# Gate vectors, scores and conditioning steps rescheduled in a two-layer mixing and expert kernel

## The chip, the cores and the metric

The kernel runs on one core of one Trainium2 chip. The metric is the device time of one execution in microseconds (us), lower is better. Engines: TensorE (PE; its weight load is PEld), VectorE (DVE), ScalarE (ACT), GpSimd (POOL) and SyncE (SP), which only issues transfers here.

## The reference, cut to what matters

Two layers over 256 tokens `x` and 256 context tokens, model width 1024, float32. In each layer a conditioning vector gives six modulation vectors (shift, scale and gate for the mixing half, the same for the expert half); the hidden state is normed and modulated, mixed (spatial gating beside a bidirectional retention with four heads), gated back into the residual, normed and modulated again, and sent through a mixture of 32 experts, two per token.

```python
def adaln(cond, w_ada, b_ada):
    m = silu(cond) @ w_ada + b_ada                 # 1024 -> 6 x 1024
    return split(m, 6)                             # sh1, sc1, gt1, sh2, sc2, gt2

def hybrid_layer(x, xc, ...):                      # xc only up to the last layer but one
    h = modulate(rmsnorm(x, g_mix), sh1, sc1)
    x = x + gt1 * token_mix(h @ w_in, ...)
    h2 = modulate(rmsnorm(x, g_ffn), sh2, sc2)
    return x + gt2 * hier_moe(h2, ...)

def token_mix(p, ...):
    u, va, q, k, vr, gr, ga, gb = split_projection(p)
    y_a = spatial_gating(gelu(u), gelu(va), ...)
    o = layernorm(retention_bidirectional(q, k, vr, ...))   # per head of 256
    y_b = silu(gr) * o
    return (sigmoid(ga) * (y_a @ w_pa) + sigmoid(gb) * (y_b @ w_pb)) @ w_out
```

## The kernel before

Weights of the mixing half come in pieces of 512 KB (`piece`, `piece_wide`, `piece_qk`, `piece_vg`, lines 237 to 260), one after the other in the order of `plan` (line 556). Each piece is split by `split_w` (line 202) into a rounded high part on ACT (line 206) and a low part on DVE (line 207), and every product is three matmuls (`mm3`, lines 264 to 266). `take` (line 300) keeps three pieces loaded and split ahead of the one in use; the pools of raw, high and low parts have three buffers each. A piece is consumed by a half of `feat_major` or `tok_major` or by a quarter of `tok_wide`, and after each of them `tick` (line 215) is called. `tick` counts, runs the functions that `defer(n, fn)` (line 222) put n ticks ahead, and then pops one conditioning step from `background` unless the count is a multiple of 8 (layer 0) or of 2 (layer 1). Layer 0 has 74 ticks: 4 for the rest of the gating values, 8 for `u`, 16 for `ga` and `w_pa` (ticks 13 to 28), 6 for each of four heads (29 to 52), 16 for `gb` and `w_pb`, 6 for `w_out`.

A conditioning step (`ada_steps`, line 419) multiplies a raw tile of `w_ada` (512 KB) by a column of the conditioning vector and adds it on DVE (line 436), once for each of one or two streams. Raw tiles are requested by the step before (`ada_raw`, line 368): one ahead up to tick 24 and in layer 1, two ahead otherwise in layer 0. Eight steps make one of the twelve vectors (l, v); then a bias row is loaded, four small matmuls sum over partitions (line 445), and vectors 2 to 5 are stored to DRAM from GpSimd's queue (line 460).

In a head, `feat_major` computes q and k, DVE and POOL rotate them (lines 854 to 857), ACT and POOL split them (`split_act`, lines 355 to 357); then `tok_wide` computes the values and the gate gr in four pieces. `scores` is deferred from before `tok_wide`: 2 ticks for head 0 of layer 0, else 1. `values` runs one tick and `back` (the transposes of the head's result) three ticks after `tok_wide`. `values` takes mean and variance of the product in PSUM, 1/sqrt on POOL (`rsqrt`, line 184), normalises on DVE (line 900) and multiplies by silu(gr) on POOL (line 902).

After `w_pb`, `w_out` is applied to two column blocks at once by `tok_wide`, the third by `tok_major`, the fourth tile by tile (`out_tile`, line 1037). For each column block pc, `residual` (line 974) multiplies by the gate vector, adds to the residual, multiplies by the scale and squares. The two vectors come from DRAM, broadcast over partitions, by `mod_slices` (line 536), two tiles in layer 0 and one in layer 1. `route_piece` (line 1003) transposes a block of the result, evicts it on ACT (line 994) and adds the router's logits (line 1000). `pump` (line 272) issues expert weights ahead, in fixed buffers.

PE and SP run their instructions in program order everywhere; DVE, ACT and POOL in program order from the `routing` section on (from the `w_pb` loop), and elsewhere in an order that a planner draws at compile time. SP waits in that order for the buffer of each load. The small tiles of pool t2 share seven buffers, those of a4 seven, those of u4 thirty.

Of the kernel before, what the change touches and what calls it, by code (L numbers as in the profile page):

```python
# [16 lines left out]
AF = mybir.ActivationFunctionType  # L17
# [24 lines left out]
PRE = (({29: 1, 52: 1, 55: 1, 57: 1, 60: 1, 62: 2, 64: 1, 68: 2, 76: 1}, 5, 9),  # L42
       ({4: 1, 8: 2, 12: 1, 18: 1, 33: 1, 38: 1, 47: 1, 50: 2, 58: 1, 59: 1, 60: 1, 61: 1, 63: 1, 65: 1, 73: 1, 74: 1, 75: 1}, 2, 12))
VA_FIRST = [(0, 0), (0, 1), (1, 0), (1, 1), (1, 2), (1, 3), (0, 2), (0, 3)]
RING = (25, 35)
KEPT = [dict(zip((*range(a, a + 5), *range(b, b + 4)), ("raw", "raw", "raw") + 3 * ("whi", "wlo"))) for a, b in ((12, 19), (24, 29))]
KEPT[1].update({8: "a4", 9: "a4", 10: "a4"})
# [4 lines left out]
def hybrid_kernel(  # L52
# [41 lines left out]
    def after(inst, gate):  # L94
        if gate is not None:
            tc.add_manual_dep(inst.ins, gate.ins.name,
                              mybir.DependencyInfo(mybir.DependencyClass.Sync, mybir.DependencyReason.DATA), reason="gate")
# [117 lines left out]
    def tick():  # L215
        ticks[0] += 1
        while deferred and deferred[0][0] <= ticks[0]:
            deferred.pop(0)[1]()
        if background and ticks[0] % (2 if layer[0] else 8):
            background.pop(0)()  # L220

    def defer(n, fn):
# [259 lines left out]
    def ada_planned(vectors):  # L482
        for l, v in vectors:
            background.extend(ada_steps(l, v))
            nexts.extend((l, v, k) for k in range(KD))

    ada_planned([(0, v) for v in range(2, 6)] + [(1, v) for v in range(4)])


    rc = const.tile([P, 2, 36], F32, name="rc")  # L490
# [42 lines left out]

    ms = {}

    def mod_slices(l, pc, gate=None):
        r = []
        for i in range(1 if l == depth - 1 else 2):
            tl = t2t((P, 2, 256))
            after(nc.sync.dma_start(tl, ada_d[l][i].rearrange("(v n) -> v n", v=6)[2:5:2, pc * 256:(pc + 1) * 256].partition_broadcast(P)), gate)  # L540
            r.append(tl)
        return r

# [28 lines left out]
    for l in range(depth):  # L572
# [121 lines left out]
        else:  # L694
# [33 lines left out]
            defer(13, between.close)  # L728
            defer(14, lambda: load_router(1))
            def ada_rest():  # L730
                ada_planned([(1, 4), (1, 5)])
                raws.append(ada_raw(*nexts.pop(0), a4t))

            defer(15, ada_rest)
# [100 lines left out]
        for h in range(HEADS):  # L835
# [45 lines left out]
            def values(scs=scs, yb=yb, vh=vh, vl=vl, gr=gr):  # L881
                st = small([P, 4, 6], tag="ost")
                mv = small([P, 4, 2], tag="omv")
                rs = small([P, 4], tag="ors")
                for s in range(ns):
                    kts = range(4) if s == 0 else range(2)
                    o = bank()
                    for tt in range(2):
                        for kt in kts:
                            sh, sl = (scs[2 * s + kt // 2][:, part, kt % 2, tt * P:(tt + 1) * P] for part in range(2))  # L890
                            vk = kt if s == 0 else 2 + kt
                            mm3(o[:, tt * DV:(tt + 1) * DV], sh, sl, vh[:, vk], vl[:, vk], kt == 0, kt == kts[-1])
                    for tt in range(2):
                        V.bn_stats(st[:, 2 * s + tt], o[:, tt * DV:(tt + 1) * DV])
                        V.bn_aggr(mv[:, 2 * s + tt], st[:, 2 * s + tt])
                    V.tensor_scalar(out=rs[:, 2 * s:2 * s + 2], in0=mv[:, 2 * s:2 * s + 2, 1], scalar1=EPS, scalar2=None, op0=ALU.add)
                    rsqrt(rs[:, 2 * s:2 * s + 2], rs[:, 2 * s:2 * s + 2])
                    for tt in range(2):
                        t = 2 * s + tt
                        V.tensor_scalar(out=yb[:, t], in0=o[:, tt * DV:(tt + 1) * DV], scalar1=mv[:, t, 0:1], scalar2=rs[:, t:t + 1],  # L900
                                        op0=ALU.subtract, op1=ALU.mult)
                        G.tensor_tensor(out=yb[:, t], in0=yb[:, t], in1=gr[:, t], op=ALU.mult)

            def back(h=h, yb=yb):
                for f in range(2):
# [2 lines left out]
                        T.transpose(o[:, t * P:(t + 1) * P], yb[:, t, f * P:(f + 1) * P], ident)  # L908
                    split_act(yT[2 * h + f][0], yT[2 * h + f][1], o[:, 0:nq], V)

            defer(1 if h or last else 2, scores)
            os_, _ = tok_wide(vgj)
            for t in range(4):
                split_act(vh[:, t], vl[:, t], os_[t][:, 0:DV], V)
# [59 lines left out]
        def residual(pc, ts, os_, ms):  # L974
            cs = slice(pc * 256, (pc + 1) * 256)
            for t, o in zip(ts, os_):
                V.tensor_tensor(out=o, in0=o, in1=ms[t // 2][:, 0], op=ALU.mult)
            for t, o in zip(ts, os_):
                done = V.tensor_tensor(out=res[t][:, cs], in0=res[t][:, cs], in1=o, op=ALU.add)
            for t, o in zip(ts, os_):  # L980
                (G if pc < 3 else V).tensor_tensor(out=h2[t][:, cs], in0=res[t][:, cs], in1=ms[t // 2][:, 1], op=ALU.mult)
            for t, o in zip(ts, os_):
                S.activation(o, res[t][:, cs], AF.Square, accum_out=ssq[:, t, pc:pc + 1])
            return done

        def turned(pc, ts):

# [29 lines left out]

        os_, _ = tok_wide([(mT[t // 2], t % 2 * P, 512) for t in range(nt)])
        for pc in range(2):
            done = residual(pc, range(nt), [o[:, pc * 256:(pc + 1) * 256] for o in os_], ms[l, pc])  # L1020
            if pc == 0:
                ms[l, 2] = mod_slices(l, 2, done)
        waiting = []
        defer(1, lambda: waiting.append(route_piece(0)))
        defer(2, lambda: waiting.pop(0)())
# [637 lines left out]
```

## Time and profile before

| | us |
|---|---|
| median of 3 runs | 1876.41 |
| lowest and highest | 1876.13 and 1877.71 |
| profiled execution | 1878.55 |
| its span, first to last instruction | 1876.5 |

In the profiled execution PE was busy for 1806.3 us (96%), PEld 1195.0, DVE 916.4, ACT 582.7 and POOL 405.8. Matmuls are pipelined, and a matmul that runs at half clock is busy for longer, so the share of PE says little about its idles; these are read from its timeline. A row of a timeline gives start, duration, engine, line, operation, output and input, and in brackets the idle of that engine just before and what ended it. Rows of windows give, for a stretch of time, the busy time and instruction count of PE, PEld, DVE, ACT and POOL, the granted clock of PE as a share of full speed, the busy share of the transfer engines and their GB/s.

### The profile page before, as it was taken

To read this page: it belongs to the slowest core of one execution; us is meant where nothing else is said; L and a number is where in the kernel's file an instruction comes from. 1 tells how busy PE (TensorE), PEld (TensorE's weight loads), DVE (VectorE), ACT (ScalarE), POOL (GpSimd) and SP (SyncE) were. 2 spreads that over 40 slices of the span, in tenths; PEclk is the share of its full clock that TensorE was granted. 3 is DMA by queue.
4 is the path that set the end of the run, shared out by engine and by line. 5 is a ranking of instruction groups with operands and counts; after the bars stand their busy time and mean duration, and the time that the engine had idled before them with its cause. 6 is when DMAs were issued, how large, how long until landed. Compare 5 with 4: busy or idle time off the path is not lost. (4 is left out here: it accounts for less than half of the span.)

```text
span 1876.5 us, 26226 instructions
## 1 busy us (share of the span) xinstructions
PE 1806.3 (96%) x9975; PEld 1195.0 (64%) x9975; DVE 916.4 (49%) x1582; ACT 582.7 (31%) x955; POOL 405.8 (22%) x372
## 2 busy tenths in 40 slices
PE   7999998999979999999999899999989999999996
PEld 4888886888875454554544599889964444444442
DVE  4878697774654424333332576755643222223223
ACT  3433233432242221121212365444432222222222
POOL 1021023310030424232333340221021112112121
PEclk8999999999989999999999999989989999999998
DMA  9545453455677999999999478634688999999996
GB/s 348 172 146 201 155 169 124 135 195 198 191 259 282 407 409 408 409 408 409 409 408 407 156 228 288 202 113 144 224 328 342 409 408 409 409 409 409 408 409 252
DMA packets 228468, 553.34 MB, mean 295 GB/s; under 512 B 23633, under 2 KB 106737, under 8 KB 228338
## 3 DMA queue, kind: packets, MB, share of 16 engines
q1 hardware_dynamic: 227954, 551.57, 78.8%
q8 instruction: 80, 1.31, 0.3%
q14 instruction: 50, 0.41, 0.1%
q0 software_dynamic: 384, 0.05, 0.0%
HBM read 550.45 MB, written 1.10 MB: 294 GB/s over the span
## 5 line engine op out<-in xcount | busy, mean ns | idle before, releaser
L1338 POOL TENSOR_TENSOR u<-u,t 128x512 f32<-128x512 f32 x184 | 230.4, 1288 | 720.4 <-DVE t L1337 720.4
L1296 PE MATMUL mm<-u,a 128*64 128x512 f32 x1376 | 334.4, 593 | 2.6 <-ACT a L1211 1.4
L207 DVE TENSOR_TENSOR wlo<-raw,whi 128x1024 fp32r<-128x1024 f32 x159 | 201.3, 1269 | 169.4 <-ACT whi L206 166.9
L266 PE MATMUL mm<-u,wlo 128*128 128x256 f32 (+1 forms) x800 | 268.3, 335 | 1.9 <-DVE wlo L207 1.9
L264 PE MATMUL mm<-u,whi 128*128 128x256 f32 (+1 forms) x800 | 269.8, 337 | 0.0
L1323 DVE SCALAR_TENSOR_TENSOR a<-mm,sw,a 64x512 fp32r<-64x512 f32 x128 | 95.9, 749 | 355.7 <-ACT a L1322 355.5
L265 PE MATMUL mm<-u,whi 128*128 128x256 f32 (+1 forms) x800 | 267.9, 335 | 0.0
L206 ACT ACTIVATE whi<-raw 128x1024 fp32r<-128x1024 f32 x160 | 169.4, 1065 | 259.1 <-PE mm L265 104.8
L1296 PEld LDWEIGHTS mm<-u,a 128*64 128x64 f32 x1376 | 105.8, 137 | 198.2 <-issue 174.2
L264 PE MATMUL mm<-whi,u 128*128 128x512 f32 (+1 forms) x496 | 181.3, 366 | 1.7 <-ACT u L607 1.0
L265 PE MATMUL mm<-wlo,u 128*128 128x512 f32 (+1 forms) x496 | 178.9, 361 | 0.0
L266 PE MATMUL mm<-whi,u 128*128 128x512 f32 (+1 forms) x496 | 178.6, 360 | 0.0
L1300 DVE TENSOR_TENSOR t<-mm,t 64x512 f32<-64x512 f32 x64 | 43.7, 683 | 272.9 <-ACT t L1299 272.9
L266 PEld LDWEIGHTS mm<-u,wlo 128*128 128x128 f32 x800 | 152.2, 190 | 18.1 <-DVE wlo L207 2.7
L1322 ACT ACTIVATE a<-mm,sw 64x512 fp32r<-64x512 f32 x128 | 87.4, 683 | 245.1 <-PE mm L1313 193.7
L264 PEld LDWEIGHTS mm<-u,whi 128*128 128x128 f32 x800 | 152.3, 190 | 17.2 <-issue 1.2
L265 PEld LDWEIGHTS mm<-u,whi 128*128 128x128 f32 x800 | 152.3, 190 | 14.6
L1313 PE MATMUL mm<-u,t 128*64 128x512 f32 x664 | 153.8, 598 | 0.5 <-ACT t L1307 0.5
L1299 ACT ACTIVATE t<-mm 64x512 f32<-64x512 f32 x64 | 38.1, 595 | 296.3 <-PE mm L1296 296.3
L1337 DVE TENSOR_TENSOR t<-mm,u 128x512 f32<-128x512 f32 x190 | 118.5, 675 | 3.4 <-POOL u L1338 3.3
L264 PEld LDWEIGHTS mm<-whi,u 128*128 128x128 f32 x496 | 95.9, 193 | 19.1 <-issue 3.7
L266 PEld LDWEIGHTS mm<-whi,u 128*128 128x128 f32 x496 | 95.2, 192 | 14.3 <-DVE u L609 0.5
(311 smaller groups left out, 2492.3 us busy)
## 6 DMA issues: line engine op xcount, KB each, us to landing
u<-in_w_dram SPq DMA_DIRECT2D x510, 512.0 KB, 10.2
raw<-in_w_dram SPq DMA_DIRECT2D x75, 512.0 KB, 10.2
whi<-in_w_dram SPq DMA_DIRECT2D x73, 512.0 KB, 9.6
wlo<-in_w_dram SPq DMA_DIRECT2D x73, 512.0 KB, 8.8
raw<-in_w_in_dram SPq DMA_DIRECT2D x64, 512.0 KB, 5.1
a<-in_w_ada_dram SPq DMA_DIRECT2D x52, 512.0 KB, 6.1
raw<-in_w_in_dram SPq DMA_DIRECT2D x96, 256.0 KB, 3.1
u<-in_w_ada_dram SPq DMA_DIRECT2D x44, 512.0 KB, 5.9
```

The costliest lines, as they stand in the source:

```text
L206: S.activation(hi, rv, AF.Copy)
L207: low_by[0].tensor_tensor(out=lo, in0=rv, in1=hi.bitcast(F32), op=ALU.subtract)
L264: T.matmul(out, lhsT=sh, rhs=mh, start=first, stop=False)
L265: T.matmul(out, lhsT=sh, rhs=ml, start=False, stop=False)
L266: return T.matmul(out, lhsT=sl, rhs=mh, start=False, stop=last)
L1296: T.matmul(o[h * 64:(h + 1) * 64, :], lhsT=x[:, s0:s0 + 64], rhs=w(k), start=(k == 0), stop=(k == KD - 1), tile_position=(0, 64 * h))
L1300: V.tensor_tensor(out=hh[0:64], in0=o[0:64, :], in1=hh[0:64], op=ALU.mult)
L1313: T.matmul(o[n % banks][n * 64:(n + 1) * 64, :], lhsT=hTt[:, s], rhs=wc(s)[:, n * 512:(n + 1) * 512], start=(s == 0), stop=(s == 3), tile_ ...
L1322: S.activation(dh, src, AF.Copy, scale=w)
L1323: V.scalar_tensor_tensor(out=dl, in0=src, scalar=w, in1=dh.bitcast(F32), op0=ALU.mult, op1=ALU.subtract)
L1337: V.tensor_tensor(out=y, in0=o, in1=g2[t // 2][:, hs], op=ALU.mult)
L1338: eng.tensor_tensor(out=res[t][:, hs], in0=res[t][:, hs], in1=y, op=ALU.add)
```

## The change

Four edits. (1) `scores` is always deferred by 2 ticks. (2) In `values` DVE subtracts the mean and multiplies by silu(gr) in one operation that reads PSUM, and ACT multiplies by 1/sqrt afterwards; POOL's multiply goes. (3) The gate and scale vectors of the third column block are loaded from GpSimd's queue after both first residuals; before, SP's queue loaded them with a wait on the first residual. (4) In layer 0 the number of conditioning steps at each tick comes from a table `ADA`, and vector (1, 2) is computed in layer 1.

```diff
+ADA = {t: 1 for t in (*range(1, 8), *range(9, 29), *(29 + 6 * h + i for h in range(4) for i in (1, 4, 5)), *range(53, 61), *range(61, 70, 2))}
+ADA.update({16: 2, 20: 2, 24: 2, 28: 2})
@@ def tick
-        if background and ticks[0] % (2 if layer[0] else 8):
+        for _ in range(min(len(background), ticks[0] % 2 if layer[0] else ADA.get(ticks[0], 0))):
             background.pop(0)()
@@
-    ada_planned([(0, v) for v in range(2, 6)] + [(1, v) for v in range(4)])
+    ada_planned([(0, v) for v in range(2, 6)] + [(1, v) for v in (0, 1, 3)])
@@ def mod_slices
-    def mod_slices(l, pc, gate=None):
+    def mod_slices(l, pc, eng=None):
-            after(nc.sync.dma_start(tl, ada_d[l][i].rearrange(...)[2:5:2, pc * 256:(pc + 1) * 256].partition_broadcast(P)), gate)
+            (eng or nc.sync).dma_start(tl, ada_d[l][i].rearrange(...)[2:5:2, pc * 256:(pc + 1) * 256].partition_broadcast(P))
@@ def ada_rest
-                ada_planned([(1, 4), (1, 5)])
+                ada_planned([(1, 2), (1, 4), (1, 5)])
@@ def values
-                        V.tensor_scalar(out=yb[:, t], in0=o[:, tt * DV:(tt + 1) * DV], scalar1=mv[:, t, 0:1], scalar2=rs[:, t:t + 1],
-                                        op0=ALU.subtract, op1=ALU.mult)
-                        G.tensor_tensor(out=yb[:, t], in0=yb[:, t], in1=gr[:, t], op=ALU.mult)
+                        V.scalar_tensor_tensor(out=yb[:, t], in0=o[:, tt * DV:(tt + 1) * DV], scalar=mv[:, t, 0:1], in1=gr[:, t],
+                                               op0=ALU.subtract, op1=ALU.mult)
+                        S.activation(yb[:, t], yb[:, t], AF.Copy, scale=rs[:, t:t + 1])
@@
-            defer(1 if h or last else 2, scores)
+            defer(2, scores)
@@ output projection
         for pc in range(2):
-            done = residual(pc, range(nt), [o[:, pc * 256:(pc + 1) * 256] for o in os_], ms[l, pc])
-            if pc == 0:
-                ms[l, 2] = mod_slices(l, 2, done)
+            residual(pc, range(nt), [o[:, pc * 256:(pc + 1) * 256] for o in os_], ms[l, pc])
+        ms[l, 2] = mod_slices(l, 2, G)
```

## Rows read from the trace of the kernel before

**Rows 1.** The page: PE's busy tenths and transferred GB/s in forty slices of 46.9 us

```profile
PE   7999998999979999999999899999989999999996
GB/s 348 172 146 201 155 169 124 135 195 198 191 259 282 407 409 408 409 408 409 409 408 407 156 228 288 202 113 144 224 328 342 409 408 409 409 409 409 408 409 252
```

**Rows 2.** Timeline of PE, 260 to 320 us (layer 0, heads 0 and 1), main idles

```profile
282.54 0.33 PE L908 MATMUL mm<-ident,u 128*128 128x128 f32 x1 [0.87 <-POOL u L902]
...
290.23 0.58 PE L264 MATMUL mm<-u,u 128*128 128x256 f32 x1 [5.24 <-ACT u L356]
291.58 0.58 PE L266 MATMUL mm<-u,u 128*128 128x256 f32 x1 [0.55 <-POOL u L357]
293.26 0.58 PE L264 MATMUL mm<-u,u 128*128 128x256 f32 x1 [0.46 <-DVE u L357]
```

**Rows 3.** Timeline of PE, 1178 to 1295 us (layer 1, heads), main idles

```profile
1219.12 0.39 PE L264 MATMUL mm<-u,u 128*128 128x256 f32 x1 [1.59 <-ACT u L356]
1220.47 0.38 PE L266 MATMUL mm<-u,u 128*128 128x256 f32 x1 [0.85 <-POOL u L357]
...
1254.34 0.39 PE L264 MATMUL mm<-u,u 128*128 128x256 f32 x1 [1.37 <-ACT u L356]
1256.10 0.58 PE L266 MATMUL mm<-u,u 128*128 128x256 f32 x1 [1.26 <-POOL u L357]
```

**Rows 4.** Timeline of PE, output projection of layer 0 and of layer 1

```profile
528.85 3.63 PE L1000 MATMUL mm<-wr,t 128*128 128x36 f32 x16 [3.64 <-ACT t L994]
...
1377.04 1.92 PE L1000 MATMUL mm<-wr,t 128*128 128x36 f32 x8 [5.00 <-ACT t L994]
```

**Rows 5.** Windows of 5 us behind these idles: after the busy times, PEclk, transfers

```profile
290.00:295.00 5.00, 3.76 (x14) 3.17 (x15) 3.85 (x5) 2.10 (x4) 1.58 (x2) 0.50 0.25 72
530.00:535.00 5.00, 5.00 (x28) 4.12 (x28) 3.34 (x7) 1.06 (x1) 0.51 (x1) 0.50 0.96 222
1223.00:1228.00 5.00, 5.00 (x26) 4.26 (x25) 3.04 (x6) 3.40 (x5) 0.13 (x1) 0.83 0.32 95
1257.00:1262.00 5.00, 5.00 (x17) 4.23 (x17) 3.94 (x7) 3.16 (x4) 0.00 (x0) 0.50 0.79 254
1376.00:1381.00 5.00, 3.96 (x19) 3.96 (x20) 3.91 (x7) 2.58 (x6) 0.51 (x1) 0.50 1.05 406
```

**Rows 6.** Timelines of POOL and ACT, layer 0, head 1

```profile
281.75 1.41 POOL L902 TENSOR_TENSOR u<-u,u 128x256 f32<-128x256 f32 x2 [0.72 <-DVE u L900]
...
289.55 0.63 ACT L356 ACTIVATE u<-t 128x512 fp32r<-128x512 f32 x1 [3.59 <-POOL t L857]
```

**Rows 7.** Window 130 to 235 us, ticks 13 to 28; its costliest DVE group

```profile
130.00:235.00 105.00, 105.00 (x504) 86.19 (x504) 77.28 (x101) 34.17 (x39) 10.88 (x12) 0.98 0.52 173
...
L436 DVE SCALAR_TENSOR_TENSOR u<-u,cst,u 128x1024 f32<-128x1024 f32 x25 | 34.2, 1399 | 0.0
```

**Rows 8.** Line 900: duration in ns, min/median/max

```profile
L900 DVE TENSOR_SCALAR u<-mm,omv,ors x24: 533/540/548, 277.1 to 1311.7; 128x256 f32<-128x256 f32 x24
```

**Rows 9.** Waits of SP's queue: us in total, times, longest

```profile
SPq L540 <- DVE mm L977: 19.0, 1, 19.0
SPq L540 <- DVE u L979: 9.6, 1, 9.6
```

**Rows 10.** Timeline of ACT, output projection of layer 0 and of layer 1

```profile
527.25 1.06 ACT L206 ACTIVATE whi<-raw 128x1024 fp32r<-128x1024 f32 x1 [7.75 <-DMA raw<-in_w_out_dram]
...
1375.45 1.06 ACT L206 ACTIVATE whi<-raw 128x1024 fp32r<-128x1024 f32 x1 [5.51 <-DMA raw<-in_w_out_dram]
```

**Rows 11.** POOL's timeline at 515 us; the page's transfer issues (KB, us to landing)

```profile
515.20 5.61 POOL L981 TENSOR_TENSOR u<-u,t 128x256 f32<-128x256 f32 x8 [44.75 <-DVE u L979]
...
u<-in_w_ada_dram SPq DMA_DIRECT2D x44, 512.0 KB, 5.9
...
ada<-t POOLq DMA_DIRECT2D x12, 4.0 KB, 2.9
```

More of the change, by code (lines that the diff above doesn't have):

```diff
@@ L539, in mod_slices @@
             tl = t2t((P, 2, 256))
-            after(nc.sync.dma_start(tl, ada_d[l][i].rearrange("(v n) -> v n", v=6)[2:5:2, pc * 256:(pc + 1) * 256].partition_broadcast(P)), gate)
+            (eng or nc.sync).dma_start(tl, ada_d[l][i].rearrange("(v n) -> v n", v=6)[2:5:2, pc * 256:(pc + 1) * 256].partition_broadcast(P))
             r.append(tl)
@@ L978, in residual @@
             for t, o in zip(ts, os_):
-                done = V.tensor_tensor(out=res[t][:, cs], in0=res[t][:, cs], in1=o, op=ALU.add)
+                V.tensor_tensor(out=res[t][:, cs], in0=res[t][:, cs], in1=o, op=ALU.add)
             for t, o in zip(ts, os_):
@@ L983, in residual @@
                 S.activation(o, res[t][:, cs], AF.Square, accum_out=ssq[:, t, pc:pc + 1])
-            return done
         def turned(pc, ts):
```

## The prediction

> **What bounds the kernel now.** I read the forty slices of the page first [rows 1]. Two regimes alternate. In the expert stages the transfers run at a flat 408 to 409 GB/s, slice after slice; nothing but fewer bytes would shorten these stretches, and the change moves hardly any bytes. In the two mixing stages (about 60 to 560 us and 1070 to 1400 us) the transfers run far below that, and TensorE is at nine tenths or more in nearly every slice. There TensorE is the bound, and the stage can only lose its idles and its slow clock. The saturated weight stream starts when the mixing stage hands over its buffers and the first expert starts, so I take a microsecond saved in either mixing stage as a microsecond of the total. Second, TensorE's timeline, only the rows with an idle in brackets: layer 0's heads [rows 2], layer 1's heads [rows 3], the output projection of both layers [rows 4]. Third, the granted clock just after those idles [rows 5]: 0.50 of full speed, that is 1.2 of 2.4 GHz, in three 5 us stretches that follow an idle of several us. So an idle costs twice: itself, and the half speed behind it.
>
> **Part 1, scores one piece later** (line 911 of the kernel before). [Rows 2] shows the idle at head 1 of layer 0: 0.87 before the transposes of head 0's result, then 5.24, 0.55 and 0.46 before head 1's scores, 7.1 us. Behind the 5.24 is a chain over ACT and POOL [rows 6]: POOL is at the old gating until 283.2, then it adds the rotary halves, and ACT's first score operand comes at 289.55. The 5 us from 290 had 3.76 us of TensorE work at 0.50, which is 1.9 us lost. In layer 1 [rows 3] has 1.59 + 0.85 at head 1 and 1.37 + 1.26 at head 2, 5.1 us; the clock costs 0.17 x 5 = 0.85 and 0.50 x 5 = 2.5, 3.4 us [rows 5]. The other heads waited for under 1 us.
> The change puts one more piece of matmuls ahead of the scores. A piece is 24 matmuls; 504 took 105 us [rows 7], 0.21 each, so a piece is 5.0 us in layer 0. In layer 1 half of a value piece's matmuls are 256 wide: about 3.8 us. Against the waits: 7.1 - 5.0 leaves 2.1 in layer 0, from which part 2 takes its share; 2.4 and 2.6 are below 3.8, so layer 1 is covered. What is late next would be the values, which need the scores' evictions: three pieces of cover remain (15 us; over 11 in layer 1). Head 0 of layer 0 has had the later place all along, and its values show no row in [rows 2]. Gain if all goes: 7.1 + 1.9 + 5.1 + 3.4 = 17.5 us. Lower end: 5.0 of the 7.1, the clock still low there, layer 1 whole: 13.5.
>
> **Part 2, values gated from PSUM** (lines 900 to 902). Per half tile of 128x256, 24 in all, it removes one DVE tensor_scalar of 0.54 us [rows 8] and one POOL multiply (two took 1.41 [rows 6], 0.7 each), and adds one DVE scalar_tensor_tensor from PSUM and one ACT copy with a scale. The trace has no scalar_tensor_tensor of exactly these operands; the same operation on 128x1024 took 1.40 [rows 7], a quarter of that is 0.35, and the removed form is 0.54. I take 0.5 (nearest in size and source), so DVE keeps its time: 24 x (0.5 - 0.54) = -1 us, between -4.6 and +1, none of it on TensorE's path alone. ACT gets 24 copies no longer than the 0.63 of a 128x512 one [rows 6]: at most 15 us in all, beside matmuls. What matters is order: DVE no longer waits for POOL's square root before it can free the bank, and POOL loses 2.8 us per head of layer 0 just ahead of the rotary adds. That is worth up to 2 us of the 2.1 left at head 1. Behind ACT's new wait for the square root stand the weight splits; they are three pieces ahead, so I cost the wait at nothing (0 to 1 us per head if that cover is gone).
>
> **Part 3, gate vectors through GpSimd's queue** (lines 540 and 1020 to 1022). The old load sits on SP's queue, which goes in program order, with a gate on the first residual. SP stood there 19.0 us in layer 0 and 9.6 in layer 1 [rows 9]. Queued behind it are the last w_out pieces. ACT's split of such a piece then waited 7.75 and 5.51 for its data [rows 10], the eviction of the router's transposes stands behind that split on ACT, and TensorE waited for that eviction 3.64 and 5.00 [rows 4]. The clock after: 0.50 x 5 = 2.5 in layer 0 and 0.50 x 3.96 = 2.0 in layer 1 [rows 5]. Gain: 3.6 + 5.0 + 2.5 + 2.0 = 13.1 us. SP's pumps of expert weights behind the gate also start some us earlier; they only refill a ring that is full before the experts start, so I count nothing.
> What it costs: three 256 KB loads (two in layer 0, one in layer 1) are now queued on POOL behind both residuals' multiplies, which in layer 0 ended at 520.8 [rows 11]. For a 256 KB load from that queue no row exists. Its bounds: the 4 KB ones landed after 2.9 us, a 512 KB load on SP's queue after 5.9 [rows 11]. I take 4.5. So in layer 0 the vectors are there at about 526.5, DVE and POOL need some 4 us for the third residual, and TensorE, freed of its idle, asks for it at about 529 to 530: 0 to 3 us late, I take 1. In layer 1 everything has half the length and half the cover: 0 to 4, I take 2. Behind the POOL instruction stands only the next residual's multiply.
> The Trainium skill speaks against this part: "DMA: Bandwidth & Descriptors", section on issuing engines that are not separate DMA queues, says that spreading issue over engines saves only the sequencer's issue time. By that rule the 13.1 would be near zero. The trace of before does not agree with it here, since SP's 19.0 us was a semaphore wait with other loads behind it, not issue.
>
> **Part 4, conditioning steps by stage** (lines 219, 487, 731). Counting ticks (one per piece, 74 in layer 0): ticks 13 to 28 get 20 steps instead of 14, the heads (29 to 52) 12 instead of 21, the rest 24 instead of 29; vector (1, 2), eight one-stream steps, goes to layer 1. A two-stream step is two DVE operations of 1.40 [rows 7], 2.8 us. So the heads lose 9 x 2.8 = 25 us of DVE work, which shortens the chain of part 1, and ticks 13 to 28 gain 6 x 2.8 = 17 us. DVE was busy 77.3 of 105 us there [rows 7], idle 27.7: it fits. But at ticks 16, 20 and 24 the second step takes a raw tile just requested, which lands 5.9 us later [rows 11], and DVE goes in order. 3 x 5.9 + 17 = 35 against 27.7: about 7 us of lateness, spread, against splits three pieces (15 us) ahead. I take 1 us on TensorE's path, bounds 0 and 8. The steps' loads move with them, 512 KB each, on SP's queue, past weight pieces; the transfers are at half load there, no cost. Layer 1 gains 8 x 1.4 = 11 us of DVE work and one small store on POOL's queue, in a stage with DVE idle: nothing.
>
> **The sum.** Gains 17.5 + 13.1 = 30.6. Given back: gate vectors late 1 + 2, double steps 1, and 2 for what part 1 leaves at head 1 or for a tile of the seven-deep t2 pool that head 0 now shares with a bias row: 6. Net 25. The profiled execution took 1878.55 us (span 1876.5 and 2.05 around it), 0.1% above the median of the runs, 1876.41; I subtract from the median: **1851.4 us**; a profile of the changed kernel would show a span near 1851.
>
> **The rivals.** (a) The gate vectors land late, or their new queue saves nothing: the output stage keeps its 13.1, heads as forecast: 1876.4 - 17.5 + 3 = 1862. (The Trainium skill's rule in part 3 would end here.) For it: no row of such a load on POOL. Against: even at 5.9 us the lateness is smaller than the idle removed. (b) The heads keep their waits, because the chain is late by DVE's order rather than by place, or because evictions come too late for the values; the output stage gains: 1876.4 - 13.1 + 3 = 1866. Against: waits of 2.4 to 2.6 us under 3.8 us of cover. (c) Slower: DVE becomes the bound in ticks 16 to 28. If at each of the three single-look-ahead double ticks the in-order wait runs as long as the queue's slow landings, about twice 5.9, and all of it reaches TensorE with the added 2.8: 3 x (11.8 + 2.8) = 44, less 6 that the sum already gives back: 1851.4 + 38 = 1889. It decides against the change from about 10 us of TensorE idle per double tick. For it: DVE at 74% there before. Against: the three-piece lead must be eaten each time. (d) The saved time is swallowed because the weight stream, not TensorE, sets the hand-over: within 0.2%. Against: the slices before each expert stage run at 113 to 342 GB/s [rows 1].
>
> **How the numbers follow.** Forecast 0.60, (a) 0.14, (b) 0.11, (c) 0.06, (d) 0.05, a better case 0.04: nothing given back, 1876.4 - 35 with the small idles and low-clock stretches that I left out = 1841. The range runs from 1841 to 1867, so it takes in (a) and (b) and leaves out (c), (d) and odd ends. A measurement of this kernel can tell about 0.2% (3.8 us) from no change. Faster by more than that: 0.60 + 0.14 + 0.11 + 0.04 = 0.89, less 0.02 for mixtures: 0.87; within: 0.06; slower: 0.07.
>
> **What would show it.** Right: no idle above 1 us before the scores in either layer, no row of SP waiting at the gate vectors' line, no idle of 3 to 5 us before the router's logits, granted clock 1.00 through the heads. Wrong: DVE waiting for w_ada tiles near 150 to 230 us with idle rows on TensorE's line 266; DVE waiting for the gate vectors before the third residual; ACT waiting for POOL's square root with a weight split behind it. The prediction fails most easily if the compiler's order of DVE, ACT and POOL, which is drawn anew outside the hand-ordered parts, opens an idle elsewhere, since an idle of 3 us costs about 5.

## The result and the profile after

The changed kernel takes 1858.18 us (median of 4 runs, 1857.55 to 1860.08) against 1877.06 for the kernel before in the same session: a ratio of 0.9895, 95% interval 0.9875 to 0.9915. That is 19 us faster, where 25 were forecast. The time lies inside the range, but it was not reached in the way of the forecast.

To see where the time went I cut both spans at the same instructions of TensorE's timeline: the first transposes for the router, the start of the experts, and their ends (us; the marks of each stage are read from the timeline).

| stage | before | after | difference |
|---|---|---|---|
| start | 44.70 | 43.73 | -1.0 |
| layer 0, mixing up to the router | 473.70 | 461.62 | -12.1 |
| layer 0, output stage | 45.48 | 49.16 | +3.7 |
| layer 0, experts | 500.26 | 500.42 | +0.2 |
| layer 1, mixing up to the router | 303.92 | 293.02 | -10.9 |
| layer 1, output stage | 32.27 | 30.56 | -1.7 |
| layer 1, experts to the end | 476.17 | 478.49 | +2.3 |
| span | 1876.5 | 1857.0 | -19.5 |

A stage can move by some 3 us without an edit in it. In the kernel with part 3 alone, described below, the mixing of layer 0 took 477.23 us and that of layer 1 300.94, 3.5 more and 3.0 less than before, though that edit stands in the output stages and the idles in the heads stayed nearly the same. What differed is the granted clock. From 150 to 200 us, where TensorE was busy throughout in both kernels, it was 0.93 against 0.97, from 250 to 300 us 0.90 against 0.93, from 1065 to 1115 us 0.93 against 0.97 and from 1215 to 1265 us 1.00 against 0.90, which adds up to about these 3.5 and 3.0 us. The sum of both mixing stages was steadier: 778.2 against 777.6.

**The heads.** The page of the changed kernel has the same two regimes as [rows 1]; PE's tenths no longer fall near 290 us, and the dip left in layer 0 is that of the output stage (here PE and GB/s in the forty slices).

```profile
PE   7999999999969999999999899999989999999996
GB/s 346 179 144 226 183 137 125 147 205 167 150 224 303 407 409 408 408 408 409 408 408 407 171 209 299 206 173 213 248 331 339 409 409 409 409 409 409 409 409 251
```

Windows of the changed kernel at the places of [rows 2, 3], with the columns of [rows 5]:

```profile
282.00:287.00 5.00, 5.00 (x27) 4.21 (x26) 2.62 (x3) 2.56 (x4) 2.04 (x3) 1.00 0.68 211
287.00:292.00 5.00, 5.00 (x32) 4.51 (x31) 4.83 (x7) 1.79 (x2) 0.00 (x0) 1.00 0.32 103
1215.00:1220.00 5.00, 5.00 (x30) 4.37 (x29) 3.16 (x6) 4.42 (x6) 0.00 (x0) 1.00 0.34 110
1250.00:1255.00 5.00, 5.00 (x41) 4.84 (x40) 3.87 (x7) 4.84 (x9) 1.29 (x1) 1.00 1.02 341
```

PE is busy for the whole of each window and the granted clock is 1.00. No idle of 0.35 us or more is left in the heads of either layer.

**The output stage.** TensorE still waits before the router's logits, in layer 0 for twice as long as in [rows 4], in layer 1 for less (timeline of PE):

```profile
524.87 3.63 PE L1002 MATMUL mm<-wr,t 128*128 128x36 f32 x16 [7.25 <-ACT t L996]
...
1360.47 1.08 PE L1002 MATMUL mm<-wr,t 128*128 128x36 f32 x8 [2.87 <-ACT t L996]
```

The reason is a new one. In the timelines of POOL, DVE and ACT, and in the view of line 543 (the load of the vectors, line 540 before):

```profile
506.25 1.55 POOL L543 DMA_DIRECT2D t<-ada  x2
...
517.92 0.77 DVE L980 TENSOR_TENSOR mm<-mm,t 128x256 f32<-128x256 f32 x2 [3.73 <-DMA t<-ada]
521.52 0.76 DVE L980 TENSOR_TENSOR mm<-mm,t 128x256 f32<-128x256 f32 x2 [2.83 <-DMA t<-ada]
...
522.63 0.39 ACT L986 ACTIVATE mm<-u 128x256 f32<-128x256 f32 x1 [14.61 <-DVE u L982]
524.25 1.05 ACT L996 ACTIVATE t<-mm 128x512 f32<-128x512 f32 x2
...
1350.26 0.81 POOL L543 DMA_DIRECT2D t<-ada  x1
1357.91 0.76 DVE L980 TENSOR_TENSOR mm<-mm,t 128x256 f32<-128x256 f32 x2 [3.38 <-DMA t<-ada]
...
DMA to landing us min/median/max: 7.6/11.7/14.4
```

POOL issues the loads of layer 0 from 506.25 on; they land 11.7 and 14.4 us after their issue, the one of layer 1 after 7.6, and DVE waits for them in the third residual. ACT squares that residual, and behind the squares, in ACT's program order, stands the eviction (line 996) of the second block's transposes, which have nothing to do with the third block. So TensorE waits. SP's row of [rows 9] is gone, and another has come at the same line:

```profile
SPq L543 <- POOL u L984: 13.9, 2, 12.9
```

SP now stands 12.9 us at the next load, the vectors of the fourth block, for a buffer of the t2 pool that POOL still reads. In the window from 496 to 504 us the transfers moved 2 GB/s.

### The profile page after: what moved, and what is told of

It is laid out like the page before. It is cut to its first block, busy times and chain, and to the rows that moved or that the text cites. A ratio compares the mean times of both kernels' runs of the same rounds, so it can differ in the third digit from the quotient of the medians.

```text
span 1857.0 us, 26227 instructions
## 1 busy us (share of the span) xinstructions
PE 1798.0 (97%) x9975; PEld 1190.8 (64%) x9975; DVE 916.7 (49%) x1582; ACT 590.9 (32%) x979; POOL 386.3 (21%) x351
## 5 line engine op out<-in xcount | busy, mean ns | idle before, releaser
L209 ACT ACTIVATE whi<-raw 128x1024 fp32r<-128x1024 f32 x160 | 169.5, 1065 | 203.0 <-PE mm L268 82.3
```

The lines of the kernel that those rows point to most:

```text
L209: S.activation(hi, rv, AF.Copy)
```

## The experiments

My theory after the result: (1) part 1 makes the gain; (2) part 3 costs in layer 0, because its load lands late; (3) parts 2 and 4 matter little. The rivals: that the parts need each other, that the queue is what is slow, that other loads in flight are, and that the load itself is. Stage times are taken at the marks of the table.

**Part 3 taken back.** The changed kernel with the load on SP's queue again:

```diff
...
+            done = residual(pc, range(nt), [o[:, pc * 256:(pc + 1) * 256] for o in os_], ms[l, pc])
+            if pc == 0:
+                ms[l, 2] = mod_slices(l, 2, done)
-        ms[l, 2] = mod_slices(l, 2, G)
```

> The changed kernel with part 3 taken back: the third block's gate vectors are again loaded by SP's queue behind a gate on the first residual. Theory (in the changed kernel the load from GpSimd's queue landed 7.6 to 14.4 us after its issue, so part 3 only moved the output projection's idle): the idles of before come back, about 3.6 us at the router's logits in layer 0 and 5.0 in layer 1, in place of 7.25 and 2.87, with about the same half-speed clock behind them; total 1854 to 1860, no more than 4 us from the changed kernel. Rival (part 3 gains what the prediction gave it, and something else lengthened the output stage): 10 us slower, about 1868.

Measured: 1854.6 us (1851.66 to 1855.84), ratio 0.9866 (0.9842 to 0.9889). That is 3.6 us faster than the changed kernel, though the intervals overlap. SP's waits and the old idles (timeline of PE) are back, the first of them smaller:

```profile
SPq L543 <- DVE mm L980: 19.6, 1, 19.6
SPq L543 <- DVE u L982: 9.7, 1, 9.7
...
515.59 1.98 PE L1003 MATMUL mm<-wr,t 128*128 128x36 f32 x16 [2.46 <-ACT t L997]
1352.73 1.93 PE L1003 MATMUL mm<-wr,t 128*128 128x36 f32 x8 [5.03 <-ACT t L997]
```

The output stage takes 42.54 us in layer 0 (49.16 with part 3) and 32.34 in layer 1 (30.56). So beside the other parts, part 3 costs 6.6 us in layer 0 and gains 1.8 in layer 1. How much it costs depends on part 4, as the kernel without part 4 shows below.

**Part 1 alone**, in the kernel before:

```diff
-            defer(1 if h or last else 2, scores)
+            defer(2, scores)
```

> The kernel before with part 1 alone: scores one piece later in every head. Theory (the place of the scores is what removed the heads' idles): no idle over 1 us before the scores in either layer, 17 to 22 us faster than before, about 1857. Rival (the DVE load of the conditioning steps delays the chain, and dealing them out otherwise is what helped): idles of 2 us and more stay at head 1 of layer 0, under 10 us faster, 1868 to 1874.

Measured: 1863.82 us (1862.89 to 1866.71), ratio 0.9923 (0.9900 to 0.9946), 15 us gained, under the 17 to 22 expected. The mixing of layer 0 takes 466.86 us (6.8 less) and that of layer 1 293.22 (10.7 less). In layer 0 small idles remain at head 1 (timeline of PE), the last two of them before its values; in layer 1 none remain:

```profile
279.76 0.33 PE L908 MATMUL mm<-ident,u 128*128 128x128 f32 x1 [0.54 <-POOL u L902]
288.84 0.38 PE L266 MATMUL mm<-u,u 128*128 128x256 f32 x1 [0.72 <-POOL u L357]
290.52 0.39 PE L264 MATMUL mm<-u,u 128*128 128x256 f32 x1 [0.94 <-DVE u L357]
...
311.28 0.39 PE L265 MATMUL mm<-u,u 128*128 128x256 f32 x1 [0.71 <-DVE u L357]
312.80 0.39 PE L265 MATMUL mm<-u,u 128*128 128x256 f32 x1 [0.91 <-DVE u L357]
```

**All but part 1**, the same edit undone in the changed kernel:

```diff
-            defer(2, scores)
+            defer(1 if h or last else 2, scores)
```

> The changed kernel with part 1 taken back: scores one piece after q and k, but for head 0 of layer 0. Theory (place): the idles come back in layer 1 whole, 5 us and their clock, and in layer 0 in part, 3 to 7 us; 10 to 18 us slower than the changed kernel, 1868 to 1876. Rival (DVE load and POOL's share of the chain): under 5 us slower, below 1863.

Measured: 1875.21 us (10 runs, 1873.12 to 1876.62), ratio 0.9979 (0.9968 to 0.9990). Without part 1 almost nothing is gained. Yet the mixing of layer 0 is 9.9 us shorter (463.79), while that of layer 1 is 5.3 us longer (309.18), with a new idle at head 0 (timeline of PE):

```profile
282.43 0.39 PE L267 MATMUL mm<-u,u 128*128 128x256 f32 x1 [1.00 <-ACT u L359]
...
1182.03 0.39 PE L267 MATMUL mm<-u,u 128*128 128x256 f32 x1 [3.15 <-ACT u L359]
1184.07 0.58 PE L269 MATMUL mm<-u,u 128*128 128x256 f32 x1 [1.54 <-POOL u L360]
```

Heads 2 and 3 of layer 1 wait too, 2.0 and 1.8 us. So most of the wait at head 1 of layer 0 goes in two ways: by a later place (part 1), or by a shorter chain (parts 2 and 4). Layer 1 needs the later place. What opens the idle at its head 0 was not tried; part 4 moves eight conditioning steps into this layer, which the prediction costed at nothing.

**Part 4 taken back, and part 2 taken back**, each alone, in the changed kernel; the diffs are those of the change, reversed, in `tick` and in the lists of vectors, and in `values`.

> The changed kernel with part 4 taken back: conditioning steps by the old rule, vector (1, 2) again in layer 0. Theory (part 4 shortened layer 0's heads by taking DVE work out of them and the output stage of layer 0 by ending the steps before it, and did nothing in ticks 13 to 28): 3 to 6 us slower than the changed kernel, 1861 to 1864, with idles of 0.5 to 1 us each at heads 1 and 2 of layer 0, none in layer 1. Rival (part 4 is neutral or its double steps and layer 1's extra steps cost as much as they give): within 2 us of 1858.

> The changed kernel with part 2 taken back: normalised on DVE, multiplied by the gate on POOL. Theory (with the scores a piece later and less DVE work in the heads nothing waits for this chain): within 2 us of the changed kernel, 1856 to 1860. Rival (POOL's multiplies ahead of the rotary adds still set the scores): idles of 0.5 us and more before the scores or the transposes, 4 to 8 us slower, 1862 to 1866.

Measured: 1860.27 us without part 4 (1857.26 to 1862.57, ratio 0.9904, 0.9887 to 0.9920) and 1859.23 without part 2 (1855.17 to 1861.22, ratio 0.9898, 0.9881 to 0.9914). Neither can be told from the changed kernel. The mixing of layer 0 takes 462.55 and 460.06, against 466.86 with part 1 alone. Beside part 1, part 4 removes all the small idles; part 2 removes those before the transposes and the scores and leaves two before head 1's values, 1.02 and 0.91 us. Without part 4, TensorE also waits elsewhere in the output stage of layer 0 (timeline of PE):

```profile
306.51 0.39 PE L268 MATMUL mm<-u,u 128*128 128x256 f32 x1 [1.02 <-DVE u L360]
521.43 0.69 PE L469 MATMUL mm<-ident,t 128*128 128x128 f32 x2 [5.34 <-DVE t L452]
```

That stage takes 46.10 us, 3.1 less than in the changed kernel. The last conditioning vector still falls into it, and SP stands at the load of its bias row (line 366) until after POOL has issued the gate vectors. So GpSimd's load goes first, lands after 6.0 and 8.5 us, and DVE doesn't wait for it in layer 0. With part 4 the fourth block's vectors stand there instead, SP issues them before POOL's load, and that load lands after 11.7 and 14.4. Part 4 thus takes idles out of the heads and makes part 3 dearer.

**The load early, in another pool, on SP's queue.** The third block's vectors get tiles of the a4 pool and are requested right behind the second `w_out` piece of that block, without a gate; nothing is on GpSimd's queue.

```diff
-        if kh and pc == 3:
-            ms[l, pc] = mod_slices(l, pc)
+        if kh:
+            ms[l, pc] = mod_slices(l, pc, a4t if pc == 2 else t2t)
-        ms[l, 2] = mod_slices(l, 2, G)
```

> The changed kernel with the third block's gate vectors in buffers of pool a4 instead of t2, loaded by SP's queue behind the second w_out piece of that block, with no gate and nothing on GpSimd's queue. Theory (what held SP before, and what made the load late after, is that no t2 buffer is free before the first residual; with another buffer the load is early and nobody waits for it): no wait of SP over 5 us at this line, no wait of DVE for it, no idle over 1 us before the router's logits in either layer; 9 to 14 us faster than the changed kernel, 1844 to 1849. Rival (the output stage's idles come from the saturated transfers or from the order on ACT): idles of 3 us and more stay, 1855 to 1860.

Measured: 1842.88 us (1842.03 to 1843.65), ratio 0.9806 (0.9784 to 0.9827): 15 us below the changed kernel, 36 below the kernel before. The output stages take 38.44 and 26.36 us. What is left of the idles at the router's logits and transposes (timeline of PE) and of SP's waits:

```profile
518.14 1.97 PE L1002 MATMUL mm<-wr,t 128*128 128x36 f32 x16 [0.50 <-ACT t L996]
1338.40 0.44 PE L993 MATMUL mm<-ident,u 128*128 128x128 f32 x2 [1.60 <-POOL u L984]
...
SPq L543 <- DMA ada<-t: 6.8, 1, 6.8
SPq L543 <- POOL u L984: 2.3, 1, 2.3
```

The gain that part 3 was forecast to bring exists; it comes once the vectors are there in time (requested at 482.32, DVE doesn't wait for them). SP's wait has not gone: both waits shown stand before the fourth block's vectors in layer 0, 9.1 us together where the changed kernel had 12.9, so the expectation of no wait over 5 us was wrong. Those vectors were issued at 499.50 and 502.17, and that was early enough.

**Why did the load land late? First the queue.** The load from ACT's queue instead of GpSimd's, at the same place of the program:

```diff
-        ms[l, 2] = mod_slices(l, 2, G)
+        ms[l, 2] = mod_slices(l, 2, S)
```

> The changed kernel with the third block's gate vectors issued from ACT's queue instead of GpSimd's, at the same place in the order. Theory (what is slow is not the kind of queue but the broadcast and its company): 8 to 14 us to landing in layer 0, 6 to 9 in layer 1, total within 4 us of the changed kernel. Rival (GpSimd's queue itself is slow with loads of this size): 3 to 6 us to landing, idles before the router's logits under 2 us, 5 to 9 us faster.

Measured: 1848.43 us (one run). ACT issued the loads 2 us sooner, at 504.22 and 504.72, since it didn't stand behind POOL's multiplies. DVE used the second one at 515.34, and in layer 1, issued at 1339.4, it waited until 1348.44 (timeline of DVE):

```profile
515.34 0.76 DVE L980 TENSOR_TENSOR mm<-mm,t 128x256 f32<-128x256 f32 x2 [0.58 <-DMA t<-ada]
1348.44 0.76 DVE L980 TENSOR_TENSOR mm<-mm,t 128x256 f32<-128x256 f32 x2 [4.71 <-DMA t<-ada]
```

Nine to eleven us on this queue too, so GpSimd's queue alone is not what makes the load slow. But it had a share: the output stage of layer 0 took 39.11 us instead of 49.16. Neither expectation came whole: the landing is the theory's, the gain of 10 us more than the rival's. The transfers from 506 to 508 by queue (q10 is ACT's, q1 SP's):

```profile
q10 hardware_dynamic: 226, 0.22, 33.1%
q1 hardware_dynamic: 140, 0.13, 28.3%
```

ACT's load moved beside the one in SP's queue, each at its own low rate. GpSimd's load, in the changed kernel, had its first packet only after 512, when SP's 512 KB of vectors had nearly gone.

**The weights in flight.** The pump of expert weights moved behind the output tiles, meant to keep them away from the load:

```diff
         sh2.append(tl)
-        pump(PRE[l][1])
...
-        pump(PRE[l][2])
+        pump(PRE[l][1] + PRE[l][2])
```

> The changed kernel, but the pump of expert weights that stands behind the third residual is moved behind the router's part of the output stage, so that SP issues no stream of 512 KB weight loads beside the gate vectors. Theory (the load from GpSimd's queue lands late because it shares the transfer engines with that stream): it lands within 3 to 6 us of its issue in both layers, where the changed kernel needed 11.7 and 14.4 in layer 0 and 7.6 in layer 1. Rival (broadcast loads from one row of DRAM are slow by themselves; in the changed kernel the transfers ran at 26 to 92 GB/s just after 504 us with the engines 0.1 to 0.3 busy): 9 us and more in layer 0 still. The total is of little interest, since expert weights start later.

Measured: 1854.65 us (one run), landing 8.0 to 14.3 us, DVE's waits 10.2 us. This decides nothing: SP has no other work between the two places and issued the same loads at the same moment, at 504.76, as before the edit. The weights alone were not tried again.

**What is read.** The vectors are one row of DRAM, read once for each of 128 partitions. In the next kernel GpSimd's load takes 128 distinct rows of x, pieces of the same length (the third block is then gated and scaled by rows of x); in the one after it, the two loads of the shift vector do.

```diff
-            (eng or nc.sync).dma_start(tl, ada_d[l][i].rearrange(...)[2:5:2, ...].partition_broadcast(P))
+            if eng is None:
+                nc.sync.dma_start(tl, ada_d[l][i].rearrange(...)[2:5:2, ...].partition_broadcast(P))
+            else:
+                eng.dma_start(tl, x_d[0, 0:P].rearrange("p (v n) -> p v n", v=4)[:, 0:3:2])
```

> The changed kernel, but the load on GpSimd's queue takes its 256 KB from 128 distinct rows of x instead of one row of the conditioning vectors read 128 times; the pieces have the same length. The third column block is therefore gated and scaled by wrong values. Theory A, many reads of the same DRAM row are slow by themselves: the load lands in 3 to 6 us instead of 7.6 to 14.4, DVE's 10 us of waiting for the vectors falls to under 3, the output stage of layer 0 shortens by 5 to 7 us, and the time is about 1851. Theory B, the load is slow because of what else is in flight then (the broadcast loads and weights that SP issues at the same moment): landing stays at 8 us or more, DVE still waits 7 us or more, time within 3 us of the changed kernel's 1858.

> The changed kernel, but the two 512 KB loads of the shift vector, which SP issues in the output stage at the same moment as GpSimd's load is under way, take distinct rows of x instead of one row read 128 times. The shift added before the experts is therefore wrong. Theory A (a load is slow by its own repeated reads): the gate vectors still land in 8 to 14 us, DVE waits 8 us or more, time about 1858. Theory C (broadcast loads hold each other up, since they read from the same few rows): the gate vectors land in 4 to 8 us, DVE's wait halves, the output stage of layer 0 shortens by 3 to 5 us and the time is about 1853. Theory B (any company does it): no change, as in A.

Measured: 1853.0 and 1859.24 us (one run each). With distinct rows for GpSimd's load it landed after 11.0 and 11.7 us in layer 0 and 7.6 in layer 1, and DVE waited 7.2 us (10 before); the output stage of layer 0 took 46.44 us, 2.7 less. With the shift alone nothing moved (landing 8.0 to 14.2, wait 10.1). So GpSimd's load is not slow by its own reads alone, and the shift's loads are not what holds it up.

**Part 3 alone**, in the kernel before:

> The kernel before, with the third part of the change alone: the gate vectors of the third block through GpSimd's queue behind both first residuals. The prediction's sum: 1877 less 13.1 plus 3 for lateness, 1867. The reading of the runs so far, that the load lands 8 to 14 us after its issue and DVE then waits for it: the idles before the router's logits in layer 0 go, but the third residual is late by as much; output stage of layer 0 from 45.5 to 48 to 52, of layer 1 from 32.3 to about 30.5, time 1877 to 1882, no faster than before.

Measured: 1878.81 us (10 runs, 1876.92 to 1881.26), ratio 0.9992 (0.9982 to 1.0001): nothing gained. The output stages took 46.18 and 31.40 us, 0.7 more and 0.9 less than before. In layer 0 the idle before the router's logits is gone, but another has come (timeline of PE), with SP's waits from 496 to 530 us:

```profile
536.42 0.69 PE L466 MATMUL mm<-ident,t 128*128 128x128 f32 x2 [5.95 <-DVE t L449]
...
SPq L363 <- DVE mm L977: 11.1, 1, 11.1
SPq L363 <- POOL t L362: 7.9, 1, 7.9
```

SP stood 19.0 us at line 363, the bias row of the last conditioning vector. The last `w_out` piece was queued behind it, DVE stood 9.55 us for the split of that piece, and the conditioning step that TensorE waited for stood behind it on DVE. For the gate vectors DVE did not wait in layer 0; in layer 1 it did, 4.1 us. So in layer 0 the idle went as expected, but the stage grew by less and for another reason: the third residual was held up by SP's next wait, not by the landing.

In layer 0 this kernel shows the load with the transfer engines nearly to itself. Its issue on POOL's timeline, then the transfers from 522.7 to 531 by queue (packets, MB, busy share of the 16 engines; q0 is GpSimd's, q1 SP's), then line 540 (the 8.4 is layer 1's):

```profile
522.71 1.57 POOL L540 DMA_DIRECT2D t<-ada  x2
...
q0 software_dynamic: 154, 0.52, 71.9%
q1 hardware_dynamic: 108, 0.11, 4.3%
...
DMA to landing us min/median/max: 6.3/8.4/8.5
```

In a cut of the same view by single microseconds the first packets come after 524, so some 1.5 us pass up to there, and the 512 KB then take until 531: some 75 GB/s with hardly any company. The 4.5 us of the prediction could not have held even here.

**All vectors from distinct rows**, on SP's queue as on GpSimd's, gate, scale and shift (all three are then rows of x):

```diff
-    (eng or nc.sync).dma_start(tl, ada_d[l][i].rearrange(...)[2:5:2, ...].partition_broadcast(P))
+    (eng or nc.sync).dma_start(tl, x_d[0, 0:P].rearrange("p (v n) -> p v n", v=4)[:, 0:3:2])
-            nc.sync.dma_start(tl, ada_d[l][i, 3 * D:4 * D].partition_broadcast(P))
+            nc.sync.dma_start(tl, x_d[0, 0:P])
```

> The changed kernel, but every load of gate and scale vectors, on SP's queue and on GpSimd's, and both loads of the shift vector take distinct rows of x instead of one row read 128 times, with pieces of the same length. The residuals are therefore gated, scaled and shifted by wrong values. In the traces so far the 512 KB of the fourth block's vectors, first in SP's queue from 504 us on, moved at 58 to 88 GB/s, and the first packet of GpSimd's load came only about 6 us after its issue. Theory A, one row read 128 times is what is slow: from 504 on SP's queue moves over 200 GB/s, GpSimd's load has its first packet within 3 us and lands within 6, DVE waits under 4 us in all, the output stage of layer 0 takes 40 to 43 us instead of 49, and the time is about 1849. Theory D, the slowness comes from the size of the pieces (1 KB) or the crowd after 504, whatever is read: SP's queue still moves 58 to 100 GB/s up to 510, the landing stays at 8 us or more, DVE waits 7 us or more, and the time is 1852 to 1858.

Measured: 1846.72 us (one run), output stage of layer 0 38.54 us instead of 49.16. The windows from 504 to 510, first of the changed kernel, then of this one (last column GB/s, before it the busy share of the transfer engines):

```profile
504.00:506.00 2.00, 2.00 (x19) 2.00 (x18) 0.21 (x2) 1.97 (x8) 2.00 (x4) 1.00 0.20 58
506.00:508.00 2.00, 2.00 (x19) 2.00 (x18) 1.38 (x1) 2.00 (x3) 1.79 (x3) 1.00 0.33 84
508.00:510.00 2.00, 2.00 (x19) 2.00 (x18) 1.23 (x1) 0.02 (x1) 0.00 (x0) 1.00 0.94 60
```

```profile
504.00:506.00 2.00, 2.00 (x20) 2.00 (x19) 0.65 (x1) 1.97 (x5) 2.00 (x4) 1.00 0.56 150
506.00:508.00 2.00, 2.00 (x19) 2.00 (x19) 1.33 (x2) 1.38 (x2) 1.15 (x2) 1.00 0.99 330
508.00:510.00 2.00, 2.00 (x19) 2.00 (x18) 0.64 (x1) 0.00 (x0) 0.00 (x0) 1.00 1.00 301
```

The loads went out at the same moments (SP 502.91 and 503.55, POOL 505.61 and 506.25), and SP stood before them for as long. But the fourth block's vectors, first in SP's queue, moved at 58 and 84 GB/s in the first four us when they were one row read 128 times, at 150 and 330 when they were distinct rows, and GpSimd's load, whose first packets came after 512 in the changed kernel, had them after 509. In layer 0 DVE no longer waited. In layer 1 it still did, 4.4 us, and the load still took 7.7 us. There the transfers were already at 418 GB/s when it was issued (1337 to 1340 us), so in layer 1 company, not the row, is the likelier cause; that was not taken apart. The landing of 6.9 to 7.7 us, above the 6 that theory A gave, points to company in layer 0 too: the first packet, after 509, was over 3 us behind the issue.

Two things limit what this shows. The edit changes the tensor that is read as well, x in place of the vectors that the kernel has stored. And repetition as such need not be slow: next in SP's queue stand the two loads of the shift vector, also one row read 128 times and from the same tensor, but in pieces of 4 KB. In the changed kernel SP's queue moved from 512 to 514 us (packets, MB, busy share):

```profile
q1 hardware_dynamic: 163, 0.59, 72.5%
```

That is 295 GB/s.

## Why the prediction was right and wrong

**A microsecond of mixing is one of the total:** held. The expert stages of all kernels stayed within 0.4 us in layer 0 and within 2.4 in layer 1. The 2.3 us that layer 1's experts lost in the changed kernel were 0.1 to 2.2 in the others whose work is complete; I have no cause for them.

**Part 1: right in mechanism, and lucky in its sum.** 17.5 us were forecast; alone it took 6.8 and 10.7 us off the two mixing stages, together 17.5, of which 15 reached the total. The split was off: 9.0 for layer 0, 8.5 for layer 1 in the forecast. What remained at head 1, 2.1 us by the forecast, showed as 0.54, 0.72 and 0.94 us. Three terms were less firm than the sum looks. A piece is 5.5 us and not 5.0, since 84 of the 504 matmuls of [rows 7] are short ones of other lines (445, 466, 496 and 801), and the 420 of lines 264 to 266 took 0.23 each. The cover of three pieces for the values did not quite hold without part 4: 0.71 and 0.91 us of idle with part 1 alone. And the 3.4 us of clock in layer 1 were no fixed price of those idles. With part 3 alone the idles at heads 1 and 2 of layer 1 were 1.60, 0.85, 1.38 and 1.26 us, those of [rows 3], but the five us behind them were granted 1.00 where [rows 5] has 0.83 and 0.50:

```profile
1227.00:1232.00 5.00, 5.00 (x29) 4.38 (x28) 3.74 (x7) 4.97 (x7) 0.00 (x0) 1.00 0.28 87
1259.00:1264.00 5.00, 5.00 (x32) 4.50 (x31) 4.07 (x7) 3.99 (x6) 0.00 (x0) 1.00 0.81 274
```

**Parts 2 and 4 in the heads: too small.** With them layer 0's mixing fell by 5.2 us more (466.86 to 461.62), where 2 were allowed for and 3 were given back elsewhere. The prediction said that 25 us of DVE work leave the heads and shorten the chain, and then gave this no number. The durations held: 24 of the new DVE operation and 24 ACT copies (lines 903 and 905; ns, min/median/max), against 0.5 us taken and 0.63 as a bound.

```profile
L903 DVE SCALAR_TENSOR_TENSOR u<-mm,omv,u x24: 466/473/481, 270.3 to 1291.3; 128x256 f32<-128x256 f32 x24
L905 ACT ACTIVATE u<-u,ors x24: 493/502/512, 271.7 to 1292.7; 128x256 f32<-128x256 f32 x24
```

ACT stood 37.1 us for POOL's square root before line 905, in 12 waits, and no idle of TensorE followed: the cover named there held. So did that of the double steps. In the window of [rows 7] DVE's work rose from 77.3 to 90.1 us of 105, and PE stayed busy for all of it:

```profile
130.00:235.00 105.00, 105.00 (x505) 86.36 (x504) 90.11 (x114) 33.56 (x39) 10.60 (x14) 0.98 0.59 200
```

Rival (c) did not come. The heads thus brought 23.0 us where 14.5 were forecast (17.5, less 1 and 2).

**Part 3: the step that failed.** The forecast was 13.1 gained and 3 given back. The two output stages together lost 2.0 us, and alone the part changed nothing (0.9992). In the changed kernel the mis-sized term is the landing of the 256 KB load: 4.5 us taken, between 2.9 and 5.9; 7.6 to 14.4 measured, 6.3 and 8.5 with hardly any company (layer 0 of part 3 alone). The rest of that step held. On the clock of the kernel before (the output stage starts 13.05 us earlier), POOL's issue came at 519.3 where 520.8 was expected, and TensorE ran out of work at 530.7 where 529 to 530 was; but the vectors came at 531 and 534.6 instead of 526.5. The upper bound was wrong in kind: the 5.9 us of [rows 11] are of a weight tile, whose 512 KB are distinct rows in pieces of 4 KB, and the vectors are one row read 128 times, in pieces of 1 KB.

The second error was to think of SP's wait as removed. It moved by one load: 19.0 us at the third block's vectors became 12.9 at the fourth's, and the transfers, idle up to 504, then met all that had piled up. With part 3 alone it became 11.1 and 7.9 at the bias row, and in layer 0 that wait, not the landing, took the gain. Rival (a) named this outcome for the output stage, "their new queue saves nothing"; its total, 1862, was 4 us too high because the heads gave more.

The Trainium skill's rule, "DMA: Bandwidth & Descriptors", section "Issuing engines are not separate DMA queues", had part 3 near zero, and alone it came out at zero. What it says of shared transfer engines on which loads interleave agrees with ACT's queue (226 packets beside 140 of SP's in the same 2 us), and with GpSimd's from 512 on; up to then GpSimd's load stood behind SP's 512 KB. That issue time is all another queue can save does not agree: the 19.0 us were a semaphore wait, which did go from SP, and from ACT's queue the same load, issued 2 us sooner, shortened the output stage by 10 us, as it moved beside SP's and not behind it. What kept part 3 from a gain was the landing and SP's next wait. The Trainium skill's fit for loads from GpSimd's queue (the same page, section "Anatomy of one DMA — SWDGE (gpsimd) path", 2.0 us plus the bytes at 436 GB/s) would give an estimate of 2.6 us for 256 KB; the measured 6.0 to 14.4 decide.

After the 7.25 us idle the clock behaved as in [rows 5]: the stretch from 525 to 530 was granted 0.50, that is 1.2 of 2.4 GHz. In the kernel with the early load, with 0.50 us of idle there, it was 1.00 from 520 to 525. "An idle costs twice" held for these long idles, and not for the short ones of layer 1 with part 3 alone.

```profile
525.00:530.00 5.00, 5.00 (x25) 5.00 (x25) 0.37 (x2) 1.26 (x4) 0.66 (x1) 0.50 0.80 319
```

**Open:** the cause of the late landing in layer 1; the fourth block's vectors by distinct rows alone, which the last kernel makes the likeliest cause in layer 0 but which were not tried by themselves; and whether it is the repetition in pieces of 1 KB or the tensor that makes them slow.

## What to carry to other kernels

When a load is taken out of a queue where it blocks, look at the next load in that queue: if it waits for buffers that free at the same moment, the block only moves. Size a load's landing by a row of the same kind of access: a broadcast by a broadcast with pieces of the same length. Vectors that are known long before they are needed are best requested early, into a pool that doesn't make the queue wait: here that was worth 15 us more than GpSimd's queue. And before a few us of a stage are put down to an edit, compare the granted clock of that stage in both kernels.

## What the runs showed of the hardware that I had not expected

Loads of one DRAM row to 128 partitions, in pieces of 1 KB, moved at 58 and 84 GB/s on SP's queue from 504 to 508 us while the transfer engines were busy for only 0.20 to 0.33 of the time, at 60 GB/s from 508 to 510 with the engines busy for 0.94, and at some 75 GB/s on GpSimd's queue with hardly any company. With distinct rows of another tensor in pieces of the same length the first four us moved 150 and 330 GB/s, and loads of one row in pieces of 4 KB 295. What in the chip makes the difference, no run here shows.

The granted clock differed between two kernels in stretches in which TensorE was busy without a break: 0.97 before and 0.93 with part 3 alone from 150 to 200 us, 1.00 with part 1 alone. What sets it there, no run here shows.
